# Later places for the normalising, mixing and evacuation of the value chunks, and for two small rows of a decoder layer

## The chip, the cores and the metric

One core of one Trainium2 chip runs the whole layer in one program. The metric is the device time of that program in microseconds. Three runs of the kernel before gave 907.71, 907.95 and 909.17 us, median 907.95.

## The reference

One sequence of 2048 positions with 1024 features goes through one layer:

```
h   = rmsnorm(x, g_pre) * (1 + scale) + shift            # shift, scale, gate from c
u, v, gg, rq, rk, rv, rg = split(h @ w_in)               # seven parts of 512 columns
y_gmlp = u * (tril(W_s) @ layernorm_groups(v) + b) * silu(gg)   # per chunk of 128 positions
y_ret  = groupnorm(retention(rotary(rq), rotary(rk), rv)) * silu(rg)
out = x + gate * rmsnorm(concat(y_gmlp, y_ret) @ w_out, g_post)
```

Layer norm of v takes 4 groups of 128 columns; W_s is a causal 128x128 matrix for each group, applied to the positions inside a chunk. `gate` is a row of 1024 numbers, made from c and a third of w_ada. All of it is float32.

## The kernel before

The sequence is done in two halves of 1024 positions (8 chunks each). Each large product is done as three TensorE products of high and low parts (`mm3`, lines 208 to 210), so each weight block and each activation is first split: ScalarE casts the high part (`wh`, `sh`, `yh`, `hh`), and VectorE subtracts it to get the low part (`wl`, `sl`, `yl`, `hl`). One `mm3` is one step. A half goes through these stages:

1. Retention values, then two passes of queries and keys, a chunk at a time in 8 steps (`token_unit`). `ret_pair` puts the retention of each chunk on the steps behind it: rotate (VectorE), add (GpSimd, L471), transposes `tp` (TensorE, L476), and so on. In half 0 the first four chunks start `6 + 4 * c` steps into the pass.
2. The gMLP values, 8 chunks of 8 steps (`pv`). `v_small` puts five things on the steps behind each chunk: statistics (VectorE, L396 and L398, from PSUM), the root (four small GpSimd instructions, L238, L239, L402, L403), the normalising (four ScalarE instructions, L408, `vh`), the mixing (TensorE, L414, `mx`: four products of 128x128, eight instructions) and its evacuation `into_y` (VectorE, L419, from PSUM). From chunk 2 on, `sums` prepares the sums of activations that stage 3 needs: 32 pieces on VectorE's list (L613, L616, and the splits L601 on ScalarE with L602 on VectorE) and 8 sums on GpSimd (L613), at steps given by SUMS_V and SUMS_G.
3. Six units (`unit`, products X, Y, Z) for the gates and u by a scheme with seven products in place of eight: 28 steps a unit. Weights are split by `pump`, one at the start of each product, more in the last unit; some weight blocks are made on GpSimd (L193, `ut`) first. In half 0 `gate_row` runs beside the units from unit 1 on: four column blocks, each with eight loads `wgt` (SyncE), eight multiply-adds (VectorE, L927 and L929), a split (L936, L937), a `spread` over the partitions (TensorE, L942, `gps`), two loads `gp` and two VectorE operations (L952, L953). The tiles of it share three buffers. In the last unit of half 0, `diag` (VectorE, ten instructions, L250 to L255) and `row` (TensorE, L273, `rb_ps`) spread the 1/rms of half 1's positions; two times, for four chunks each.
4. The output product (`out_unit`, `z`, L967 to L969), 16 steps a chunk. Half 1's h is built beside that of half 0.

The order is written out by hand. `Slots` holds a list of functions by step: `slots.at(d, fn)` puts fn at d steps from now, and `tick`, called ahead of every step, issues what is due. Functions due at the same step are issued in the order in which they were put there. TensorE, VectorE, ScalarE and GpSimd execute their instructions in just this order; a step is thus a place in four queues, not a moment, and an engine that waits for nothing runs ahead of TensorE's steps. `mx`, `gps`, `rb_ps` and `tp` stand in TensorE's queue between the steps: if their input is late, everything behind them on TensorE is late as well.

Of the kernel before, what the change touches and what calls it, by code (L numbers as in the profile page):

```python
# [30 lines left out]
QT = QUAD * P  # L31
XBUF = (9, 3)
OUT_LATE = 8
SUMS_V = ((), (), (1, 3, 4, 5, 6), (1, 3, 4, 5, 6, 7), (1, 3, 4, 5, 6), (1, 3, 4, 5, 6, 7),
          (1, 3, 4, 5, 6), (1, 3, 5, 6, 7))
SUMS_G = ((), (), (0, 5), (4, 6), (4, 6), (4, 6), (), ())
OCH = (4, 5, 6, 7, 0, 1, 2, 3)
V_PUMPS = ((),) * 7 + ((1, 4),)
QK_PUMPS = ((), (), (1,), (1,), (1,), (1,), (1, 4), (1, 4))
# [55 lines left out]
def tile_hybrid_layer(ctx: ExitStack, tc, x, xt, wm, wg, win, wun, wout, wst, cols, rows, pos, cst,  # L95
# [10 lines left out]
    slots = Slots()  # L106
# [29 lines left out]
    def slot(name, shape=(512,), dtype=F32):  # L136
        return big.tile([P, *shape], dtype, name=name, tag="s")
# [99 lines left out]
    def rsqrt_eps(rs, ms, n=1):  # L237
        G.tensor_scalar(rs, ms, 1.0, EPS, ALU.mult, ALU.add)  # L238
        G.tensor_tensor(rs, rs, nhalf[:, 0:n], ALU.pow)  # L239
# [18 lines left out]
    def xpart(half, ch, hf):  # L258
        row = half * HALF + ch * P
        xx = slot("xp")  # L260
        SP.dma_start(xx, x[row:row + P, hf * 512:(hf + 1) * 512])
        jk = slot("xj", dtype=BF16)
        S.activation(jk, xx, AF.Square, scale=1.0 / 32.0, accum_out=ss2[:, hf, ch:ch + 1])
# [21 lines left out]
    def xdma(half, q, kb):  # L285
        t = slot("xt")
        SP.dma_start(t, xt[half * 2 + q, kb])
        return t
# [95 lines left out]

    yT, yR = {}, {}

    def v_small(half, ch, ps, when=(0, 1, 4, 8, 10)):
        mv = small.tile([P, GROUPS, 2], F32, name="mv", bufs=4)
        st = small.tile([P, GROUPS, 6], F32, name="st")
        rs = small.tile([P, GROUPS], F32, name="rsv", bufs=4)  # L390
        nb = small.tile([P, GROUPS], F32, name="nbv", bufs=4)
        box = {}

        def stats():
            for g in range(GROUPS):
                V.bn_stats(st[:, g, :], ps[:, g * P:(g + 1) * P])  # L396
            for g in range(GROUPS):
                V.bn_aggr(mv[:, g, :], st[:, g, :])  # L398

        def root():  # L400
            rsqrt_eps(rs, mv[:, :, 1], GROUPS)
            G.tensor_tensor(nb, mv[:, :, 0], rs, ALU.mult)  # L402
            G.tensor_scalar(nb, nb, -1.0, 1.0, ALU.mult, ALU.mult)  # L403

        def norm():
            vh = box["vh"] = slot("vh", (GROUPS, P))
            for g in range(GROUPS):
                S.activation(vh[:, g, :], ps[:, g * P:(g + 1) * P], AF.Identity,  # L408
                             bias=nb[:, g:g + 1], scale=rs[:, g:g + 1])

        def mix():
            mx = box["mx"] = ps_s.tile([P, GROUPS, P], F32, name="mx", tag="sm")
            for g in range(GROUPS):
                T.matmul(mx[:, g, :], box["vh"][:, g, :], wst_t[:, g, :], start=True, stop=True)  # L414

        def into_y():
            y = yT[half, ch // QUAD]
            for g in range(GROUPS):
                V.scalar_tensor_tensor(y[:, ch % QUAD, g, :], box["mx"][:, g, :],  # L419
                                       cols_t[:, 32 + g:33 + g], bs_b[:, g, :], ALU.mult, ALU.add)  # L420

        for t, fn in zip(when, (stats, root, norm, mix, into_y)):
            slots.at(t, fn)
# [273 lines left out]
    def token_unit(half, ps_i, ch, name, pumps=(1,), pool=None):  # L697
        ps = ps_m.tile([P, 512], F32, name=name, tag="m")
        for kb in range(KB):
            slots.tick()  # L700
            if kb in pumps:
                pump()
            mm3(ps, hchunk(half, ch, kb), blocks[half * PER_HALF + ps_i * KB + kb], kb == 0,
                kb == KB - 1)
        return ps
# [208 lines left out]
    def gate_row(mp):  # L914
        W = 256

        def tile_(name, dtype=F32):
            return mp.tile([P, W], dtype, name=name, tag="w", bufs=3)

        def part(kc, c):  # L920
            a, s1 = gg[:, c * W:(c + 1) * W], sc[:, kc:kc + 1]
            w = tile_("wgt")
            SP.dma_start(w, wg[kc, :, c * W:(c + 1) * W])

            def add():
                if kc == 0:
                    V.tensor_scalar(a, w, s1, None, ALU.mult)  # L927
                else:
                    V.scalar_tensor_tensor(a, w, s1, a, ALU.mult, ALU.add)  # L929

            slots.at(5, add)

        def halves(c):
            a = gg[:, c * W:(c + 1) * W]
            ag[c] = tile_("ah", F32R), tile_("al", F32R)
            S.copy(ag[c][0], a)  # L936
            V.tensor_tensor(ag[c][1], a, ag[c][0].bitcast(F32), ALU.subtract)  # L937

        def spread(c):
            gps[c] = ps_s.tile([P, 512], F32, name="gps", tag="sm")  # L940
            for n in range(2):
                T.matmul(gps[c][:, 0:W], ones_r, ag[c][n], start=n == 0, stop=n == 1)  # L942

        def params(c):
            gp[c] = [tile_("gp") for _ in range(2)]
            for n, t in enumerate(gp[c]):
                at = 512 + n * D + c * W
                SP.dma_start(t, rows[0:1, at:at + W].partition_broadcast(P))

        def end(c):  # L950
            a = gg[:, c * W:(c + 1) * W]
            V.tensor_tensor(a, gps[c][:, 0:W], gp[c][0], ALU.add)  # L952
            V.tensor_tensor(a, a, gp[c][1], ALU.mult)  # L953

        gps, gp, ag = {}, {}, {}
        for c in range(D // W):
            for kc in range(KB):
                slots.at(30 * c + 2 * kc, lambda kc=kc, c=c: part(kc, c))
            for t, fn in ((21, halves), (23, spread), (24, params), (30, end)):
                slots.at(30 * c + t, lambda fn=fn, c=c: fn(c))  # L960

    hb = {}

# [68 lines left out]
    def opened(name):  # L1032
        areas.append(tc.tile_pool(name=name, bufs=1, reuse_waits="tile"))
        return areas[-1].__enter__()
# [10 lines left out]
    qk = {}  # L1045
    for half in range(2):

        if half == 0:
# [3 lines left out]
            rp = opened(f"ret{half}")  # L1052
            table_inputs()
            qk = second_quad(rp, *first)
            for n, fn in enumerate(tables(half, rp)):
                slots.at(n + 2, fn)
        for ch in range(QUAD if half == 0 else 0, NCH):
            ps = token_unit(half, 0, ch, "prv", () if half == 0 else (1,))
            rv_small(half, ch, ps)
            if half == 1 and ch == 2:  # L1060
                closed(3)
                y_tiles("yR", half, yR)
                rp = opened(f"ret{half}")
# [4 lines left out]
        for pr_ in range(2):  # L1068
            early = half == 0 and pr_ == 0
            if early:  # L1070
                for c in range(QUAD):
                    ret_pair(rp, half, pr_, c, qk[c], 6 + 4 * c)
            for ch in range(QUAD if early else 0, NCH):
                if half == 0 and pr_ == 1:
                    for hf in range(2):
                        slots.at(2 + 4 * hf, lambda ch=ch, hf=hf: xpart(1, ch, hf))
                pumps = QK_PUMPS[ch] if pr_ else (1, 4) if early else (1,)
                ps = token_unit(half, 1 + pr_, ch, "pqk", pumps)
                ret_pair(rp, half, pr_, ch, ps, 30 - 4 * ch if early else 0)
# [4 lines left out]
        for ch in range(NCH):  # L1084
            if ch == 2:
                closed()
                y_tiles("yT", half, yT)
                up = opened(f"unit{half}")
                on_v, on_g, late = sums(half, up)
            for t in SUMS_V[ch]:  # L1090
                slots.at(t, on_v.pop(0))
            for t in SUMS_G[ch]:
                slots.at(t, on_g.pop(0))
            ps = token_unit(half, 3, ch, "pv", V_PUMPS[ch])
            v_small(half, ch, ps)


        for un in range(len(UNITS)):
            if un == 0:
                for n, fn in enumerate(late):  # L1100
                    slots.at(1 + 3 * (n // 2) + n % 2, fn)
            if un == 1 and half == 0:
                gate_row(up)
            if un == len(UNITS) - 1:
                slots.at(16, lambda: ysplit(half, OCH[0], 0))
                slots.at(27, lambda: ysplit(half, OCH[0], 1))
            if un == len(UNITS) - 1 and half == 0:
                for q in range(2):
                    def diag(q=q):
                        hb["dg", q] = xdiag2(rs2[:, q * QUAD:(q + 1) * QUAD])  # L1110

                    def row(q=q):
                        hb[q] = xrow(hb["dg", q])

                    slots.at(10 + 6 * q, diag)
                    slots.at(13 + 6 * q, row)

                hb["x"] = []
                for n in range(2):
                    slots.at(24, lambda n=n: hb["x"].append(xdma(1, 0, n)))  # L1120
            unit(half, un, up)
# [82 lines left out]
```

## Time and profile before

| | us |
|---|---|
| median of three runs | 907.95 |
| the profiled execution | 909.25 |
| its span, first to last instruction | 907.5 |
| TensorE (PE) busy | 870.1 |
| VectorE (DVE) busy | 603.7 |
| ScalarE (ACT) busy | 294.3 |
| GpSimd (POOL) busy | 326.8 |

Times in the rows are microseconds from the start of the span. PE stands for TensorE's products, PEld for its weight loads, SPq for SyncE's queue of transfers. A row of a timeline tells in square brackets how long the engine was idle ahead of it and what ended that. `x8` is the number of instructions that a row merges. `hh` is the high, `hl` the low part of h.

### The profile page before, as it was taken

What the parts mean: (1) busy time and instruction counts of PE and PEld (TensorE: products, weight loads), DVE (VectorE), ACT (ScalarE), POOL (GpSimd) and SP (SyncE); (2) the same over time, 40 slices, a digit from 0 to 9 for tenths busy, and PEclk for the clock granted to TensorE, in tenths of its full rate; (3) what the DMA queues carried; (4) which work ended last, traced back from release to release, by engine and by line L of the source; (5) the groups of instructions that cost most, each with busy time, mean ns of one, the idle gap of its engine ahead of it and who ended that gap; (6) DMA issues with size and microseconds to landing.
All of it is one profiled execution on the core that took longest, in us unless ns stands there. A gap on an engine that the chain in (4) does not pass through costs nothing.

```text
span 907.5 us, 11911 instructions
## 1 busy us (share of the span) xinstructions
PE 870.1 (96%) x4198; PEld 717.7 (79%) x4198; DVE 603.7 (67%) x1217; ACT 294.3 (32%) x585; POOL 326.8 (36%) x399
## 2 busy tenths in 40 slices
PE   2999999999899999999999999999998999999997
PEld 1778788888688778778888888888877888888886
DVE  4989876566886777976676665466479734475332
ACT  4673223323263323433351012111124532253221
POOL 2040363356654555311110033333467554630000
PEclk9999999999999999999999999999999999999999
DMA  8961232300012333644443200110001112142222
GB/s 324 333 233 37 92 112 63 97 20 18 1 47 77 104 107 110 248 150 139 152 176 103 81 1 24 59 36 1 1 1 47 47 48 66 56 145 105 95 102 82
DMA packets 43835, 84.86 MB, mean 94 GB/s; under 512 B 5248, under 2 KB 10496, under 8 KB 43776
## 3 DMA queue, kind: packets, MB, share of 16 engines
q1 hardware_dynamic: 43776, 84.10, 27.6%
q8 instruction: 33, 0.54, 0.2%
q14 instruction: 26, 0.21, 0.1%
HBM read 75.69 MB, written 8.39 MB: 93 GB/s over the span
## 4 chain that ended last, share of the span: by engine, by line
PE 74%; DVE 11%; issue 4%; POOL 4%; DMA 3%; ACT 3%; SPq 0%; DVEq 0%; POOLq 0%; ACTq 0%
PE z L968 6%; PE z L969 6%; PE z L967 6%; PE pqk L208 6%; PE pqk L210 6%; PE pqk L209 6%; PE pY L210 3%; PE pY L209 3%; PE pY L208 3%; PE prv L210 2%; PE prv L209 2%; PE prv L208 2%; DVE wl L176 2%; PE o L509 2%; PE pX L209 2%
## 5 line engine op out<-in xcount | busy, mean ns | idle before, releaser
L208 PE MATMUL pqk<-wh,hh 128*128 128x512 f32 x240 | 102.6, 427 | 0.0
L968 PE MATMUL z<-wl,yh 128*128 128x512 f32 (+1 forms) x264 | 101.1, 383 | 0.2 <-DVE wl L176 0.2
L969 PE MATMUL z<-wh,yl 128*128 128x512 f32 (+1 forms) x264 | 101.1, 383 | 0.0
L967 PE MATMUL z<-wh,yh 128*128 128x512 f32 (+1 forms) x264 | 101.0, 383 | 0.0
L210 PE MATMUL pqk<-wh,hl 128*128 128x512 f32 x240 | 94.4, 394 | 0.0
L209 PE MATMUL pqk<-wl,hh 128*128 128x512 f32 x240 | 93.7, 390 | 0.0
L471 POOL TENSOR_TENSOR rA<-rA,rB 128x512 f32<-128x512 f32 x32 | 42.0, 1311 | 134.7 <-DVE rB L463 100.6
L176 DVE TENSOR_TENSOR wl<-wr,wh 128x512 fp32r<-128x512 f32 x94 | 84.3, 920 | 6.5 <-ACT wh L173 6.4
L485 ACT COPY qkT<-tp 128x512 f32<-128x512 f32 x32 | 18.8, 587 | 173.6 <-PE tp L476 173.6
L579 DVE SCALAR_TENSOR_TENSOR zo<-z,zrs,gg 128x512 f32<-128x512 f32 x30 | 22.4, 745 | 58.9 <-POOL zrs L574 58.9
L173 ACT CAST wh<-wr 128x512 fp32r<-128x512 f32 x96 | 55.2, 618 | 17.3 <-DMA wr<-in_win 8.6
L573 POOL TENSOR_SCALAR zrs<-zss 128x1 f32<-128x1 f32 x15 | 4.5, 303 | 148.5 <-ACT jz L570 148.5
L968 PEld LDWEIGHTS z<-wl,yh 128*128 128x128 f32 x264 | 49.6, 188 | 10.2 <-DVE wl L176 0.5
L969 PEld LDWEIGHTS z<-wh,yl 128*128 128x128 f32 x264 | 49.6, 188 | 10.0 <-DVE yl L559 0.4
L967 PEld LDWEIGHTS z<-wh,yh 128*128 128x128 f32 x264 | 49.6, 188 | 9.8
L637 POOL TENSOR_TENSOR yT<-yT,c 128x512 f32<-128x512 f32 x20 | 30.8, 1544 | 62.7 <-DVE c L658 38.7
L210 PEld LDWEIGHTS pqk<-wh,hl 128*128 128x128 f32 x240 | 45.0, 188 | 10.4
L208 PE MATMUL pv<-wh,hh 128*128 128x512 f32 x128 | 52.6, 411 | 0.0
L209 PEld LDWEIGHTS pqk<-wl,hh 128*128 128x128 f32 x240 | 45.5, 189 | 6.5 <-issue 0.2
L210 PE MATMUL pv<-wh,hl 128*128 128x512 f32 x128 | 50.5, 394 | 0.0
L208 PEld LDWEIGHTS pqk<-wh,hh 128*128 128x128 f32 x240 | 45.4, 189 | 6.4 <-issue 0.2
L209 PE MATMUL pv<-wl,hh 128*128 128x512 f32 x128 | 50.4, 394 | 0.0
(233 smaller groups left out, 2216.7 us busy)
## 6 DMA issues: line engine op xcount, KB each, us to landing
wr<-in_win SPq DMA_DIRECT2D x64, 256.0 KB, 3.7
ur<-in_wun SPq DMA_DIRECT2D x48, 256.0 KB, 3.2
slab<-in_wm SPq DMA_DIRECT2D x16, 512.0 KB, 6.7
wr<-in_wout SPq DMA_DIRECT2D x32, 256.0 KB, 4.7
xr<-in_x SPq DMA_DIRECT2D x16, 512.0 KB, 3.4
out<-xr SPq DMA_DIRECT2D x32, 256.0 KB, 2.0
xt<-in_xt SPq DMA_DIRECT2D x24, 256.0 KB, 4.5
xp<-in_x SPq DMA_DIRECT2D x16, 256.0 KB, 2.7
```

The lines of the kernel that those rows point to most:

```text
L173: S.copy(hi, r)
L176: eng.tensor_tensor(lo, r, hi.bitcast(F32), ALU.subtract)
L208: T.matmul(ps, l[0], r[0], start=first, stop=False, skip_group_check=reopened)
L209: T.matmul(ps, l[0], r[1], start=False, stop=False, skip_group_check=reopened)
L210: T.matmul(ps, l[1], r[0], start=False, stop=last, skip_group_check=reopened)
L471: G.tensor_tensor(A, A, box["B"].rearrange("p g h d -> p (g h d)"), ALU.add)
L485: S.copy(qkT, box["tp"])
L579: V.scalar_tensor_tensor(zo, z[c], rs, gg[:, cs], ALU.mult, ALU.mult)
L637: eng.tensor_tensor(y, y, by, ALU.mult)
L967: T.matmul(z, l[0], r[0], start=f, stop=False)
L968: T.matmul(z, l[0], r[1], start=False, stop=False)
L969: T.matmul(z, l[1], r[0], start=False, stop=e)
```

## The change

Numbers in schedules change, nothing else; the instructions are the same.

- `v_small`: normalising at step 7 in place of 4, mixing at 12 in place of 8, `into_y` at 14 in place of 10, counted from the chunk's end. The mixing of a chunk thus goes from the start of the next chunk but one to its middle (step 4 of it).
- SUMS_V: pieces of the sums at steps 1 to 5 (with 7) in place of 1 and 3 to 7. SUMS_G: in two chunks of four the GpSimd sums move from steps 4 and 6 to 5 and 7.
- `gate_row`: 33 steps a block in place of 30; spread at 25 in place of 23, loads `gp` at 26 in place of 24, end at 32 in place of 30.
- `ret_pair` of the first four chunks of half 0: one step later.
- `row` of the roots: 5 steps behind its `diag` in place of 3.

```diff
-SUMS_V = ((), (), (1, 3, 4, 5, 6), (1, 3, 4, 5, 6, 7), (1, 3, 4, 5, 6), (1, 3, 4, 5, 6, 7),
-          (1, 3, 4, 5, 6), (1, 3, 5, 6, 7))
-SUMS_G = ((), (), (0, 5), (4, 6), (4, 6), (4, 6), (), ())
+SUMS_V = ((), (), (1, 2, 3, 4, 5), (1, 2, 3, 4, 5, 7), (1, 2, 3, 4, 5), (1, 2, 3, 4, 5, 7),
+          (1, 2, 3, 4, 5), (1, 2, 3, 5, 7))
+SUMS_G = ((), (), (0, 5), (4, 6), (5, 7), (5, 7), (), ())
...
-    def v_small(half, ch, ps, when=(0, 1, 4, 8, 10)):
+    def v_small(half, ch, ps, when=(0, 1, 7, 12, 14)):
...
-                slots.at(30 * c + 2 * kc, lambda kc=kc, c=c: part(kc, c))
-            for t, fn in ((21, halves), (23, spread), (24, params), (30, end)):
-                slots.at(30 * c + t, lambda fn=fn, c=c: fn(c))
+                slots.at(33 * c + 2 * kc, lambda kc=kc, c=c: part(kc, c))
+            for t, fn in ((21, halves), (25, spread), (26, params), (32, end)):
+                slots.at(33 * c + t, lambda fn=fn, c=c: fn(c))
...
-                    ret_pair(rp, half, pr_, c, qk[c], 6 + 4 * c)
+                    ret_pair(rp, half, pr_, c, qk[c], 7 + 4 * c)
...
-                    slots.at(13 + 6 * q, row)
+                    slots.at(15 + 6 * q, row)
```

## Rows read from the trace of the kernel before

**Rows 1.** The page, part 1: busy time, share of the span, instructions.
```profile
PE 870.1 (96%) x4198; PEld 717.7 (79%) x4198; DVE 603.7 (67%) x1217; ACT 294.3 (32%) x585; POOL 326.8 (36%) x399
```

**Rows 2.** Waits of PE: us in total, times, longest.
```profile
PE mx L414 <- ACT vh L408: 8.0, 6, 1.9
...
PE tp L476 <- POOL rA L471: 1.1, 1, 1.1
PE gps L942 <- DVE al L937: 1.1, 2, 0.6
PE rb_ps L273 <- DVE dgr L254: 1.0, 1, 1.0
...
PE pY L208 <- DVE u L658: 0.7, 1, 0.7
...
PE z L968 <- DVE wl L176: 0.2, 1, 0.2
```

**Rows 3.** Windows from mixing to mixing, half 0: length, PE busy, clock, DMA, GB/s.
```profile
212.14:218.49 6.35, 6.35 (x34) 1.00 0.00 0
...
240.41:249.33 8.92, 7.02 (x32) 1.00 0.00 0
249.33:257.70 8.37, 8.35 (x32) 0.80 0.13 31
```

**Rows 4.** Windows over six such stretches, each half: length, PE, PEld, DVE, ACT, POOL.
```profile
212.14:257.70 45.56, 41.60 (x193) 34.04 (x192) 38.29 (x104) 15.47 (x37) 30.48 (x33) 0.96 0.03 6
653.45:697.53 44.08, 40.05 (x193) 32.82 (x192) 38.05 (x104) 13.96 (x34) 30.52 (x33) 1.00 0.03 7
```

**Rows 5.** Timeline of DVE, value chunks of half 0: start, length, instruction, idle before.
```profile
225.85 0.97 DVE L602 TENSOR_TENSOR sl<-sj,sh 128x512 fp32r<-128x512 f32 x1 [2.42 <-ACT sh L601]
...
233.65 1.56 DVE L602 TENSOR_TENSOR sl<-sj,sh 128x512 fp32r<-128x512 f32 x2 [2.13 <-ACT sh L601]
```

**Rows 6.** Timeline of POOL, same stretch.
```profile
205.84 0.19 POOL L238 TENSOR_SCALAR rsv<-mv 128x4 f32<-128x4 f32 x1 [2.27 <-DVE mv L398]
...
207.51 0.20 POOL L403 TENSOR_SCALAR nbv<-nbv 128x4 f32<-128x4 f32 x1
...
223.73 1.29 POOL L613 TENSOR_TENSOR sj<-hh,hl 128x512 f32<-128x512 f32 x1
...
245.98 2.54 POOL L402 TENSOR_TENSOR nbv<-mv,rsv 128x4 f32<-128x4 f32 x1
```

**Rows 7.** Timeline of ACT, same stretch.
```profile
223.81 1.51 ACT L408 ACTIVATE vh<-pv,nbv,rsv 128x128 f32<-128x128 f32 x4 [4.22 <-POOL nbv L403]
```

**Rows 8.** Windows of units 1 to 5 of half 0: columns as in Rows 4.
```profile
278.80:298.51 19.71, 19.60 (x87) 15.99 (x86) 13.66 (x21) 7.22 (x13) 10.46 (x9) 1.00 0.34 108
298.51:320.23 21.72, 20.17 (x87) 15.84 (x86) 16.11 (x23) 7.22 (x13) 11.63 (x9) 1.00 0.33 105
320.23:341.03 20.80, 19.82 (x87) 15.99 (x86) 16.01 (x24) 6.72 (x12) 11.57 (x9) 1.00 0.33 105
341.03:360.08 19.05, 19.05 (x85) 15.77 (x84) 14.62 (x23) 5.55 (x10) 10.02 (x8) 1.00 0.37 119
360.08:382.05 21.97, 21.00 (x91) 16.67 (x90) 20.49 (x45) 9.13 (x17) 9.18 (x7) 1.00 0.73 264
```

**Rows 9.** Timeline of DVE, unit 2 of half 0.
```profile
311.71 0.48 DVE L929 SCALAR_TENSOR_TENSOR gg<-wgt,sc,gg 128x256 f32<-128x256 f32 x1 [2.58 <-DMA wgt<-in_wg]
312.11 0.68 DVE L658 TENSOR_TENSOR u<-pY,s 128x512 f32<-128x512 f32 x1
```

**Rows 10.** Timeline of DVE, unit 5 of half 0.
```profile
365.97 0.98 DVE L953 TENSOR_TENSOR gg<-gg,gp 128x256 f32<-128x256 f32 x1 [1.38 <-DMA gp<-in_rows]
```

**Rows 11.** Timeline of PE, first query and key chunk behind the start.
```profile
100.51 0.39 PE L210 MATMUL pqk<-wh,hl 128*128 128x512 f32 x1
...
101.19 0.39 PE L210 MATMUL pqk<-wh,hl 128*128 128x512 f32 x1
102.70 0.66 PE L476 MATMUL tp<-cst_t,rA 128*128 128x128 f32 x4 [1.12 <-POOL rA L471]
```

## The prediction

> **What bounds the kernel now.** I read the page's busy shares first: TensorE is busy 96% of the span and VectorE 67% [rows 1], so TensorE's queue is the bound, and an edit that leaves its instructions alone can only win back gaps in it. The waits of TensorE say where the gaps are [rows 2]. The largest within reach is the mixing, which waits 8.0 us on the normalised values, six times; then the spreads of the gate row (the row on `al`, and a like one on `ah`), the roots' row with 1.0, the first transposes of the retention with 1.1, and a product `pY` with 0.7. The list counts only the time ahead of a first instruction, so I take the loss from windows cut at the mixings. An undisturbed stretch from one mixing to the next is 6.35 us; the worst is 8.92, and the one behind it has 8.37 at a mean clock of 0.80 [rows 3]: TensorE fell to its lower level of 1.2 GHz for part of it, right after the longest wait. Six stretches should take 6 x 6.35 = 38.10 us. They take 45.56 in half 0 and 44.08 in half 1 [rows 4]: 7.46 and 5.98 lost, together **13.44 us**, clearly more than the 8.0 of the list.
>
> Why the mixing is late is in the other three queues. ScalarE's normalising stood 4.22 us waiting for GpSimd's `nbv` [rows 7]. Behind it stood the casts `sh`, for which VectorE then idled 2.42 and 2.13 us [rows 5]; behind VectorE stood the next chunk's statistics, thus the next root. So one late chunk makes the next one later, until the pieces of the sums run out.
>
> **The change, part by part.** A step is 0.68 us (101.19 less 100.51) [rows 11].
>
> *Value chunks.* The mixing comes four steps later, 2.72 us more for the same chain. The worst lateness is 8.92 - 6.35 = 2.57 us [rows 3], under 2.72. Normalising at step 7 also lets the casts pass ahead of it on ScalarE, so the two idle times of VectorE and the snowball go. `into_y` is needed only by unit 2's products with yT, so its four steps cost nothing; the mixing in the middle of a chunk writes a PSUM bank of its own and takes TensorE the same time. The gap gone, the clock has no reason to fall. What is late next is VectorE: it is busy 38.29 and 38.05 us in these stretches [rows 4], and they shrink to 38.10. It has no reserve; what does not fit is carried into unit 0, whose weight splits stand in the same queue. Bounds of this give-back: 0 if nothing spills; at most 4.5 us a half if the GpSimd sums that now ran in VectorE's two idle times (four of 1.29 us [rows 6], at most 2.42 + 2.13 = 4.55 of idle [rows 5]) hold VectorE up instead. Since 38.05 against 38.10 is nearly a fit, I take a value near the lower end, 1.0 a half. Sum: 13.44 - 2.0 = 11.4 us won (4.4 to 13.4).
>
> First the row, then a rule on this: a GpSimd root instruction of four columns took 2.54 us at 245.98, its kind 0.20 at best [rows 6], while VectorE was running without a pause. The Trainium skill, "SBUF — State Buffer", section "Who interferes with whom", says why: VectorE and GpSimd share one pair of ports under an exclusive lock, and whoever comes second is blocked for the whole instruction. The trace agrees in kind (2.54 against 0.20). By that rule, closing VectorE's gaps speaks against the change: every sum on GpSimd that used to fall into a gap would now stop VectorE, and the sum would be 4.4 us won in place of 11.4. It is the first rival below.
>
> *Gate row.* Unit 4 has no spread: 19.05 us. Unit 1 has one and waits nowhere by the list: 19.71, so a spread costs up to 0.66 itself. Units 2 and 3 take 21.72 and 20.80 [rows 8], hence 2.01 and 1.09 lost, 3.1 in all. In unit 2, a multiply-add waited 2.58 us for its load, with `u` behind it on VectorE [rows 9] and `pY` behind `u` on TensorE: that is the 0.7 of the list. With 33 steps a block, block 1's adds begin at step 10 of unit 2 in place of 7, the first three of them and the fourth's wait still ahead of `u`; block 2's stand behind it. The spreads fall on step 2 of unit 3, step 7 of unit 4 and step 12 of unit 5, each with 4 steps = 2.72 us between split and spread in place of 1.36; the waits for the two halves of the split are 0.6 at most each on the list [rows 2], so 1.36 more covers them. Of the loads, each multiply-add still frees the buffer for the one three places on, and SyncE stands before a load until then as it does now. Bounds 0 and 3.4 (the latter if a spread costs only 0.35, half of unit 1's excess); I take 2.7, since `pY` of unit 2 may keep a little.
>
> *Roots' row.* Two steps are 1.36 us against a wait of 1.0. But the last unit of half 0 has VectorE busy 20.49 of 21.97 us [rows 8], and block 3 of the gate row now moves into it: four multiply-adds at 0.48 [rows 9] and the split's subtraction, at most 0.98 by the other two-input row of 256 columns [rows 10], make 2.9 us ahead of `diag`. Against that, the block's end, which waited 1.38 us for its load [rows 10], goes behind `diag`, and its load then lands under other work: net at most 1.5 us later. The product `z` already waits for VectorE's splits, 0.2 [rows 2], so what VectorE loses arrives there, and the 1.0 at `rb_ps` isn't won, only moved to `z`. SyncE's load `gp` of block 3 now waits for the spread at step 12, with loads of w_out queued behind it; ScalarE's casts of these run ahead of VectorE, which covers it. Bounds: 1.0 won to 1.5 lost. No row decides between; I take 0.8 lost.
>
> *First retention chunks.* The chain rotate, add, transpose moves as a whole, so its five steps stay five. But VectorE reaches the rotation late (it is still at the tables), so the add ends when it ends, and TensorE does one step more ahead of it: of the 1.1 us wait [rows 2, 11] 0.68 goes. Chunk 4 then follows after 3 steps in place of 4, with its add now ahead of chunk 3's state on GpSimd. Bounds 0 and 0.7; I take 0.7.
>
> **Sum.** 11.4 + 2.7 - 0.8 + 0.7 = 14.0 us. The profiled execution was 909.25 us (span 907.5 and 1.75 around it): it becomes 895.25. The median of the runs is 1.30 under the profiled one, so I forecast 907.95 - 14.0 = **894.0 us**.
>
> **Rivals.**
> 1. *VectorE becomes the bound of value chunks and unit 0.* For: it is busy 38.05 of the 38.10 us that remain, and sums on GpSimd lose the idle time in which they ran. Against: ScalarE's casts no longer make it wait, and the two moved pairs of GpSimd sums fall beside `into_y` and statistics, which read PSUM. Price: 4.5 a half in place of 1.0, 7.0 in all: 901.0 us.
> 2. *The small rows give nothing.* For: the gate row's new phase makes new collisions (block 3 in the unit where VectorE is fullest). Against: twice the distance to each spread. Price: 2.7 not won and 0.7 more lost: 897.4 us.
> 3. *The change doesn't do what it says*: normalising behind the casts comes later by as much as the mixing does, and the gaps stay. Against: the normalising waits for `nbv`, not for its place in the queue [rows 7]. 907.9 us.
> 4. *Slower: the root is held up in every chunk.* The pieces of the sums now stand at steps 1 to 5, right where the root is issued. If two of its instructions are held as the longest row is, 2 x (2.54 - 0.20) = 4.68 us [rows 6], every mixing of the twelve comes 4.68 - 2.72 = 1.96 late: 23.5 us in place of 13.44, the rest as forecast (2.7 - 0.8 + 0.7 won): 907.95 + 10.1 - 2.6 = 915.4 us. Against: of the roots of half 0, one instruction alone was held that long. It decides from (13.44 + 2.6) / 12 = 1.34 us late a mixing on, a root 4.1 us longer than the undisturbed one, which runs from 205.84 to 207.71 [rows 6].
>
> **Chances.** Forecast 0.59, rival 1 0.21, rival 2 0.12, rival 3 0.03, rival 4 0.05. Faster by over 0.2% (1.8 us, about what a measurement of this kernel tells from no change) holds in the first three: 0.92; within it 0.03; slower 0.05. The range goes from 889.0 (nothing given back: 2.0, the gate row's 3.4, the roots' 1.0 won in place of 0.8 lost make 4.5 under 894.0, rounded) to 902.0, which takes in rivals 1 and 2.
>
> **What would show it.** Right: stretches between mixings near 6.35 in both halves, no wait of `mx` on `vh`, no lower clock behind chunk 5, no idle of VectorE on `sh`; units 2 and 3 under 20.2 us; unit 5 and the first `z` product no shorter than before, with `z` waiting on `wl` for longer and `rb_ps` for less; `tp` waiting about 0.4. Rival 1 would show as waits of unit 0's products on `wl` or `u`, rival 4 as root instructions of over 1 us throughout. The prediction fails if waits of `mx` remain above 3 us in all, or if TensorE's new waits on VectorE come to over 5 us.

## The result and the profile after

| | before | after |
|---|---|---|
| median, us (four runs each, one chip) | 908.56 | **895.93** |
| lowest and highest, us | 907.71 to 909.60 | 894.45 to 896.12 |
| ratio, with its 95% interval | | 0.9857 [0.984, 0.9874] |
| span of the profiled execution, us | 907.5 | 894.3 |

The change wins 12.6 us; 14.0 were forecast. The forecast time, 894.0, is 1.9 us short of the median. Two of its terms, though, were wrong by more than that, in opposite directions.

Where the span shrank is read from windows that are cut at the same four places of both kernels: first product of unit 1, first `z`, and first product of unit 1 in half 1. The columns are length, then the busy time of PE, PEld, DVE, ACT and POOL, the granted clock, the DMA share and GB/s. Before:

```profile
0.00:278.80 278.80, 255.35 (x1294) 209.94 (x1295) 206.59 (x468) 108.47 (x213) 112.27 (x162) 0.99 0.33 112
278.80:382.05 103.25, 99.64 (x433) 80.26 (x432) 80.89 (x135) 35.84 (x65) 52.87 (x38) 1.00 0.42 142
382.05:718.90 336.85, 332.38 (x1645) 275.40 (x1644) 229.57 (x486) 92.94 (x189) 104.98 (x148) 1.00 0.21 69
```

After:

```profile
0.00:270.02 270.02, 251.49 (x1294) 208.81 (x1295) 206.00 (x468) 108.26 (x213) 110.47 (x162) 1.00 0.33 116
270.02:375.38 105.36, 100.77 (x433) 81.39 (x432) 86.58 (x134) 35.95 (x65) 53.87 (x38) 0.98 0.40 133
375.38:705.75 330.37, 330.14 (x1645) 275.08 (x1644) 227.80 (x487) 92.69 (x189) 102.39 (x148) 1.00 0.22 72
```

The first and the third stretch, which hold the value chunks of the two halves, win 8.78 and 6.48 us. The second, units 1 to 5 of half 0 with the gate row and the roots' row, **loses 2.11**, although the prediction had 1.9 won there. The remainder of the span differs by 0.05.

The waits of TensorE in the kernel after (us in total, times, longest) answer to [rows 2]:

```profile
...
PE pY L208 <- DVE u L658: 1.9, 2, 1.6
PE gps L942 <- ACT ah L936: 1.6, 1, 1.6
PE gps L942 <- DVE al L937: 0.6, 1, 0.6
PE tp L476 <- POOL rA L471: 0.5, 1, 0.5
PE rb_ps L273 <- DVE dgr L254: 0.4, 1, 0.4
...
PE z L968 <- DVE wl L176: 0.2, 1, 0.2
```

No row on `mx` is left. The same six stretches from mixing to mixing as in [rows 4]:

```profile
213.81:251.88 38.07, 38.07 (x193) 32.40 (x192) 36.45 (x105) 15.27 (x36) 28.56 (x34) 1.00 0.08 27
649.54:687.62 38.08, 38.08 (x193) 32.39 (x192) 36.46 (x105) 15.29 (x36) 28.57 (x34) 1.00 0.09 29
```

TensorE is busy in every microsecond of them, at the full clock. The lengths were 45.56 and 44.08, so 7.49 and 6.00 are won, all that there was to win. The work on VectorE did not become the bound: its busy time fell from 38.29 to 36.45, and GpSimd's from 30.48 to 28.56, with one instruction more on each. So the two are busy for less time with about as much work (not quite the same: VectorE has two sums `sj` of L613 fewer, one split `sl` and two splits `wl` more). Single instructions got longer even so. The splits `sl` of half 0, before and then after (number, busy time in all, mean length in ns, idle time ahead of them and what ended it):

```profile
L602 DVE TENSOR_TENSOR sl<-sj,sh 128x512 fp32r<-128x512 f32 x7 | 5.2, 761 | 4.6 <-ACT sh L601 4.6
L602 DVE TENSOR_TENSOR sl<-sj,sh 128x512 fp32r<-128x512 f32 x8 | 7.8, 979 | 0.0
```

The idle time on `sh` is gone, as forecast.

The loss is in units 4 and 5 (windows of units 1 to 5, columns as above; before in [rows 8]):

```profile
270.02:289.30 19.28, 19.28 (x87) 16.00 (x86) 15.18 (x21) 7.22 (x13) 10.29 (x8) 1.00 0.29 100
289.30:308.50 19.20, 19.20 (x85) 15.69 (x84) 15.80 (x23) 7.13 (x13) 12.17 (x9) 1.00 0.35 112
308.50:327.78 19.28, 19.28 (x87) 16.00 (x86) 15.62 (x22) 5.07 (x9) 10.62 (x8) 1.00 0.43 118
327.78:351.48 23.70, 21.48 (x87) 17.10 (x86) 16.75 (x22) 6.48 (x12) 11.29 (x9) 0.93 0.28 89
351.48:375.38 23.90, 21.53 (x91) 16.59 (x90) 23.22 (x49) 10.03 (x18) 9.49 (x7) 1.00 0.65 232
```

Units 1 to 3 win 0.43, 2.52 and 1.52. Unit 4 loses 4.65 and unit 5 loses 1.93. Unit 4 now has block 2's spread. The timelines there show why it waits (start, length, instruction, idle before it). VectorE:

```profile
323.76 2.95 DVE L929 SCALAR_TENSOR_TENSOR gg<-wgt,sc,gg 128x256 f32<-128x256 f32 x2
327.23 2.37 DVE L929 SCALAR_TENSOR_TENSOR gg<-wgt,sc,gg 128x256 f32<-128x256 f32 x2
...
332.41 1.49 DVE L929 SCALAR_TENSOR_TENSOR gg<-wgt,sc,gg 128x256 f32<-128x256 f32 x1
334.37 0.94 DVE L937 TENSOR_TENSOR al<-gg,ah 128x256 fp32r<-128x256 f32 x1 [0.47 <-ACT ah L936]
```

GpSimd:

```profile
330.27 1.67 POOL L637 TENSOR_TENSOR yT<-yT,c 128x512 f32<-128x512 f32 x1 [0.97 <-DVE c L658]
331.90 1.72 POOL L193 TENSOR_TENSOR ut<-ur 128x512 f32<-128x512 f32 x1
333.57 1.45 POOL L193 TENSOR_TENSOR ut<-ur,ut 128x512 f32<-128x512 f32 x1
```

TensorE, and then the windows (columns as above) over the spread, right behind it and after that:

```profile
334.39 0.38 PE L942 MATMUL gps<-ah,ones 128*128 128x256 f32 x1 [1.63 <-ACT ah L936]
335.36 0.39 PE L942 MATMUL gps<-al,ones 128*128 128x256 f32 x1 [0.59 <-DVE al L937]
```

```profile
332.50:336.50 4.00, 1.78 (x8) 1.17 (x7) 2.33 (x2) 1.93 (x4) 2.52 (x2) 0.99 0.25 38
336.50:341.00 4.50, 4.50 (x14) 3.58 (x13) 2.65 (x5) 0.19 (x1) 0.00 (x0) 0.63 0.89 320
341.00:346.00 5.00, 5.00 (x23) 4.14 (x23) 1.89 (x3) 1.96 (x4) 1.30 (x1) 1.00 0.09 26
```

A multiply-add that took 0.48 us in the kernel before at its best [rows 9] takes 1.2 to 1.5 here (a row of two is read as its mean), five of them, while GpSimd is at `yT` times `c` and at the weight sums `ut`. The kernel before had such long ones in block 2 as well, but two only:

```profile
335.72 2.94 DVE L929 SCALAR_TENSOR_TENSOR gg<-wgt,sc,gg 128x256 f32<-128x256 f32 x2
```

In the kernel after the last one ends at 333.90; TensorE has been standing at the spread since 332.76. It waits 1.63 and 0.59 us, and in the next window the granted clock is 0.63: TensorE spent part of it at 1.2 GHz in place of 2.4, and 14 products pass where 4.50 us at the rate of the window behind it (5.00 us for 23) would pass 20 or 21. In unit 5 the product `pY` waits 1.6 for `u`, which stands on VectorE behind the ten `diag` instructions and block 3 of the gate row. What the longer block was to win in unit 2 is there: no multiply-add waits for its load, and `pY` does not wait for `u`.

### The profile page after: what moved, and what is told of

Same layout as the page of the kernel before. It is cut to its first block, busy times and chain, and to the rows that moved or that the text cites. A ratio compares the mean times of both kernels' runs of the same rounds, so it can differ in the third digit from the quotient of the medians.

```text
span 894.3 us, 11921 instructions
## 1 busy us (share of the span) xinstructions
PE 865.1 (97%) x4198; PEld 717.4 (80%) x4198; DVE 607.3 (68%) x1217; ACT 294.0 (33%) x585; POOL 323.8 (36%) x399
## 4 chain that ended last, share of the span: by engine, by line
PE 86%; DVE 5%; DMA 4%; issue 3%; ACT 1%; SPq 1%; POOL 0%; DVEq 0%; POOLq 0%; ACTq 0%
PE z L969 6%; PE z L968 6%; PE z L967 6%; PE pqk L210 6%; PE pqk L208 6%; PE pqk L209 6%; PE pv L208 3%; PE pv L210 3%; PE pv L209 3%; PE pY L210 3%; PE pY L209 3%; PE pY L208 3%; PE prv L210 2%; PE prv L209 2%; PE prv L208 2%
```

## The experiments

The ratio of each, with its 95% interval, is to the kernel before on the same chip. Times are medians of four to six runs. The experiments ran on four chips, where the kernel before took from 907.94 to 908.81 us, so a difference of two medians from different chips is uncertain by up to 0.9 us; where it is small, that is said. "Units 1 to 5" is the window from the first product of unit 1 to the first `z` in half 0, 103.25 before and 105.36 after.

### Which part of the change does what

**Only the value chunks** (before, with the new steps of `v_small` and the new SUMS_V and SUMS_G, as in the change's diff):

```diff
-    def v_small(half, ch, ps, when=(0, 1, 4, 8, 10)):
+    def v_small(half, ch, ps, when=(0, 1, 7, 12, 14)):
```

> The kernel before with the value chunks' part of the change alone (normalising, mixing, evacuation and the steps of the sums). Theory: this part alone wins 14.2 us, all of the stretches' loss and the waits in unit 0, so 894.3 us; units 1 to 5 as before. Rival, as I predicted it: VectorE gives 2.0 of it back, 897.2 us.

Measured: 894.00 us (893.82 to 894.41), ratio 0.9842 [0.9829, 0.9855]. This part alone wins 14.3 us, 1.9 more than the whole change. I had expected units 1 to 5 as before, but they are 0.92 us shorter. The gate row is untouched here; in its unit 2 VectorE waited 1.97 us for the load for which it waited 2.58 before [rows 9], and the wait of `pY`, 0.7 before, is not in the list. The next experiment, with the same gate row, has it again: 2.56 us for the load and 0.64 at `pY`. So this wait comes and goes. That leaves some 13.4 of the 14.3 to the value chunks, about what the stretches won in the kernel after (7.49 and 6.00). The window of units 1 to 5, and two waits that this kernel keeps from before:

```profile
270.84:373.17 102.33, 99.65 (x433) 80.26 (x432) 82.90 (x135) 35.84 (x65) 53.36 (x38) 1.00 0.43 143
```

```profile
PE tp L476 <- POOL rA L471: 1.1, 1, 1.1
...
PE rb_ps L273 <- DVE dgr L254: 1.0, 1, 1.0
```

**The change without the new gate row:**

```diff
-                slots.at(33 * c + 2 * kc, lambda kc=kc, c=c: part(kc, c))
-            for t, fn in ((21, halves), (25, spread), (26, params), (32, end)):
-                slots.at(33 * c + t, lambda fn=fn, c=c: fn(c))
+                slots.at(30 * c + 2 * kc, lambda kc=kc, c=c: part(kc, c))
+            for t, fn in ((21, halves), (23, spread), (24, params), (30, end)):
+                slots.at(30 * c + t, lambda fn=fn, c=c: fn(c))
```

> The changed kernel with the gate row's old schedule (30 steps a block, spread at 23, end at 30); all else as changed. Theory: the new schedule lost time, since units 1 to 5 of half 0 take 105.4 us in the changed kernel and 103.3 before; with the old one they go back to about 103 us or less (the roots' row keeps its two steps, worth up to 1.0), so 893 to 894 us, some 2 to 3 under the changed kernel; the waits of gps on ah (1.6) and the lower clock in unit 4 go, the waits of units 2 and 3 (2.0 and 1.1) come back. Rival, as I predicted it: the new schedule won 2.7 us, so this kernel takes about 898.6.

Measured: 892.84 us (892.27 to 893.24), ratio 0.9827 [0.9814, 0.984]: 3.1 us **faster** than the whole change. The theory that the new gate row loses holds, the prediction's own term of 2.7 won falls. (By the two ratios the loss is 2.7, and their intervals just touch.)

```profile
270.06:373.16 103.10, 99.43 (x433) 80.25 (x432) 83.08 (x134) 35.75 (x65) 53.79 (x38) 1.00 0.42 142
...
304.34 0.47 PE L208 MATMUL pY<-hh,wh 128*128 128x512 f32 x1 [0.64 <-DVE u L658]
...
367.17 0.47 PE L208 MATMUL pY<-hh,wh 128*128 128x512 f32 x1 [1.46 <-DVE u L658]
```

Against the window of the kernel after, units 1 to 5 are 2.26 us shorter. The other two rows, of the timeline of TensorE, are the wait of unit 2 just spoken of and one in unit 5: the wait of `pY` there is found with the old gate row too, so it belongs to the roots' row. Against the experiment before this one, the retention's step and the roots' row are added. Unit 1 starts 0.78 earlier (270.84 to 270.06: the retention), units 1 to 5 take 0.77 more, and what lies behind the first `z` is 0.8 shorter (519.1 to 518.3: the spans of 892.3 and 891.5 less the ends of the windows). Of the 0.77, the roots' row has 0.5 at most (the 1.0 at `rb_ps` gone, 1.46 at `pY` come); 0.64 is the wait of unit 2, which neither part touches. The two parts were not run apart.

Taken one after the other, the 12.35 us between 908.28, the before of these runs, and 895.93 are 14.3 won with the value chunks, 1.2 by retention and roots' row together, and 3.1 lost by the gate row. The 0.92 of units 1 to 5 is in the first of these figures.

### Value chunks: the sums and the place of the normalising

**The old steps of the sums** (after, with SUMS_V and SUMS_G of before; no other edit):

```diff
-SUMS_V = ((), (), (1, 2, 3, 4, 5), (1, 2, 3, 4, 5, 7), (1, 2, 3, 4, 5), (1, 2, 3, 4, 5, 7),
-          (1, 2, 3, 4, 5), (1, 2, 3, 5, 7))
-SUMS_G = ((), (), (0, 5), (4, 6), (5, 7), (5, 7), (), ())
+SUMS_V = ((), (), (1, 3, 4, 5, 6), (1, 3, 4, 5, 6, 7), (1, 3, 4, 5, 6), (1, 3, 4, 5, 6, 7),
+          (1, 3, 4, 5, 6), (1, 3, 5, 6, 7))
+SUMS_G = ((), (), (0, 5), (4, 6), (4, 6), (4, 6), (), ())
```

> The changed kernel with the old steps of the sums (SUMS_V and SUMS_G as before). Theory: the steps of the sums decide little, since a piece's place is only its order in a queue; stretches between mixings stay at 6.35 us and the time within 1 us of the changed kernel, 895 to 897. Rival: the new steps are what lets VectorE fit; without them mixings or unit 0 wait again by 2 to 4.5 us a half, 900 to 905.

Measured: 898.30 us (898.15 to 899.92), ratio 0.9893 [0.9879, 0.9907], 2.4 more than after. My theory of no more than 1 us falls; the time lies between it and the rival's 900, and what happens is what the rival said. The stretches between mixings stay whole, and the loss is behind them (window, then waits):

```profile
213.56:251.64 38.08, 38.08 (x193) 32.39 (x192) 36.51 (x98) 14.11 (x33) 25.87 (x32) 1.00 0.08 27
```

```profile
PE pY L210 <- DVE wl L176: 0.8, 2, 0.4
```

From the first mixing to unit 1 it takes 58.07 us in place of 56.21, and 1.87 more in half 1 as well. That is the give-back of rival 1: at the window's end VectorE is seven instructions behind (98 in place of 105), and carries them into unit 0, whose products wait for their split weights there. (The list names 0.8 of the 3.7 as waits on `wl`; the rest are delays in unit 0 too short or too spread out to stand in it.) The splits `sl` take 1.18 us on average here, 0.98 in the kernel after. The new steps of the sums avoid the give-back. That 3.7 us in the value stages cost only 2.4 of the time has its reason in unit 4: there the same two waits of 1.6 and 0.6 stand at the spread, but the clock stays up in this profile.

```profile
338.10:342.60 4.50, 4.50 (x21) 3.73 (x20) 2.65 (x5) 1.55 (x4) 0.87 (x1) 1.00 0.92 313
```

21 products pass in a window as long as the one in which 14 passed in the kernel after.

**Only the GpSimd sums at their old steps** (after, with SUMS_G of before):

```diff
-SUMS_G = ((), (), (0, 5), (4, 6), (5, 7), (5, 7), (), ())
+SUMS_G = ((), (), (0, 5), (4, 6), (4, 6), (4, 6), (), ())
```

> The changed kernel with the old steps of GpSimd's sums alone (two chunks at steps 4 and 6 in place of 5 and 7); VectorE's pieces as changed. Tells which of the two lists kept VectorE's work from spilling into unit 0, where the old steps of both cost 1.9 us a half. Theory: VectorE's list did it (its pieces go ahead of the evacuation that waits for TensorE's mixing), so this kernel takes 896 us as the changed one, without a wait of unit 0 on wl. Rival: GpSimd's list did it (its sums now run beside evacuation and statistics, which read PSUM, and don't hold VectorE up); then 898.3 us as with both old.

Measured: 895.51 us (894.17 to 896.27), ratio 0.9854 [0.9834, 0.9875]: as after, and no wait on `wl` in unit 0. So of the two lists, VectorE's, SUMS_V, is the one that counts.

**The normalising back at step 4, the mixing late** (after, with this edit):

```diff
-    def v_small(half, ch, ps, when=(0, 1, 7, 12, 14)):
+    def v_small(half, ch, ps, when=(0, 1, 4, 12, 14)):
```

> The changed kernel with the normalising back at step 4, the mixing left at 12 and the evacuation at 14. Theory: the casts of the sums stand behind the normalising again, so VectorE idles on sh (about 2 us, some twice a half) and its work is late for unit 0; mixings wait under 1 us in all, and the time is 1 to 4 us over the changed kernel, 897 to 900. Rival: the four steps of the mixing are all that counts, and the time is that of the changed kernel within 0.5 us, with no wait in unit 0.

Measured: 902.11 us (898.54 to 903.75), ratio 0.9925 [0.9908, 0.9942]; 6.2 worse than after. The direction held, the price was larger, and its place was another than I had named: no mixing waits, but unit 0 does, on a copy of ScalarE's. The waits of TensorE, then ScalarE's timeline:

```profile
PE pX L208 <- ACT s L673: 3.7, 2, 1.9
```

```profile
255.01 1.51 ACT L408 ACTIVATE vh<-pv,nbv,rsv 128x128 f32<-128x128 f32 x4 [2.49 <-POOL nbv L403]
...
256.91 0.61 ACT L673 COPY s<-pX 128x512 f32<-128x512 f32 x1
```

In the kernel after, the copy at 253.09 runs ahead of the last normalising at 254.08. So the late place is needed for the normalising itself too: ScalarE stands at it until the root is there, and whoever is behind it is late. What the waits do not cover of the 6.2 follows the clock: the run of 898.54 us has a mean of 0.999, that of 903.75 one of 0.993.

### The gate row: length of a block and place of its spread

Two kernels fill the table of the two numbers that the change altered. **Block of 30 with the late spread**, the rest as after:

```diff
-                slots.at(33 * c + 2 * kc, lambda kc=kc, c=c: part(kc, c))
-            for t, fn in ((21, halves), (25, spread), (26, params), (32, end)):
-                slots.at(33 * c + t, lambda fn=fn, c=c: fn(c))
+                slots.at(30 * c + 2 * kc, lambda kc=kc, c=c: part(kc, c))
+            for t, fn in ((21, halves), (25, spread), (26, params), (30, end)):
+                slots.at(30 * c + t, lambda fn=fn, c=c: fn(c))
```

> The changed kernel with 30 steps a block in the gate row as before, but its spread at 25 and its loads gp at 26 as changed (end at 30). Tells the block's length apart from the spread's distance. Theory: the length did the harm (it puts block 2's last multiply-add and split at the start of unit 4, where GpSimd is busiest) and the distance helps: the waits of gps on ah and al in units 2 and 3 (about 1.0 each with spread at 23) go, units 1 to 5 take 101 us in place of 103.1, the time is 891 us. Rival: the distance does nothing, since the split comes as much later as it may; 892.8 us, as with the old schedule.

**Block of 33 with the early spread** (and its `params` and `end` as before), the rest as after:

```diff
-            for t, fn in ((21, halves), (25, spread), (26, params), (32, end)):
+            for t, fn in ((21, halves), (23, spread), (24, params), (30, end)):
```

> The changed kernel with 33 steps a block in the gate row, but spread at 23, loads gp at 24 and end at 30 as before. Theory: the length of 33 does the harm, and with two steps less the wait of gps in unit 4 is 1.4 us longer (about 3 on ah), units 1 to 5 take 106 to 108 us, the time is 897 to 898. Rival: the distance did the harm (loads gp behind the spread hold up the queue of transfers), so the time falls to 893.

Measured, with the two kernels that were there already (the block's end is at 32 in the kernel after and at 30 in the other three):

| | spread at 23 | spread at 25 |
|---|---|---|
| block of 30 steps | 892.84 | 890.89 (890.46 to 891.98), ratio 0.9811 [0.9797, 0.9824] |
| block of 33 steps | 899.42 (898.69 to 900.05), ratio 0.9902 [0.9888, 0.9916] | 895.93 |

Both expectations held in the time, the second with 1.4 us more than I had; with the block of 30 one spread still waits 0.5 on `al`. The distance wins 2.0 at the one length and 3.5 at the other; the longer block loses 5.0 or 6.6. Block of 33, spread at 23, the longest wait of all of them:

```profile
PE gps L942 <- ACT ah L936: 4.3, 2, 3.0
```

**Is it GpSimd that makes the multiply-adds long?** After, with three products `yT` times `c` of unit 3 in half 0 on VectorE in place of GpSimd; each costs VectorE 0.69 us. The products with `c21` and `c12` get the same condition as this one:

```diff
-        slots.at(0, lambda: used(half, kind, pair, up, tmp["c22"], 1, 1, False))
+        slots.at(0, lambda: used(half, kind, pair, up, tmp["c22"], 1, 1, False, half == 0 and un == 3))
```

> The changed kernel with three multiplications of yT by u in unit 3 of half 0 (128x512, 1.5 to 1.7 us each on GpSimd, around the start of unit 4) moved from GpSimd to VectorE, where such a one takes about 0.7. Adds 2 us to VectorE's own work, takes 4.8 from GpSimd. Theory: VectorE's multiply-adds of the gate row's block 2 were long (about 1.5 us in place of 0.48) because GpSimd ran beside them, so with fewer GpSimd instructions there the split is ready sooner: the wait of gps on ah in unit 4 falls from 1.6 to under 0.8 and the lower clock goes, 893 to 895 us. Rival: the multiply-adds are late by their place in VectorE's queue; 2 us more work ahead of them makes the wait 2 us longer, 898 us.

Measured: 891.95 us (891.43 to 892.52), ratio 0.982 [0.9804, 0.9836], 4.0 less than after. VectorE has more instructions, and the block is ready earlier:

```profile
327.62 1.00 DVE L929 SCALAR_TENSOR_TENSOR gg<-wgt,sc,gg 128x256 f32<-128x256 f32 x2
...
330.94 0.48 DVE L929 SCALAR_TENSOR_TENSOR gg<-wgt,sc,gg 128x256 f32<-128x256 f32 x1
331.88 0.43 DVE L937 TENSOR_TENSOR al<-gg,ah 128x256 fp32r<-128x256 f32 x1 [0.47 <-ACT ah L936]
```

The same instructions as in the kernel after take 1.00 for two in place of 2.37, 0.48 in place of 1.49 and 0.43 in place of 0.94, and no spread waits. GpSimd is idle beside them, for 10.78 us up to this row:

```profile
336.87 1.30 POOL L637 TENSOR_TENSOR yT<-yT,sg 128x512 f32<-128x512 f32 x1 [10.78 <-ACT sg L645]
```

That settles it: the length of the multiply-adds was GpSimd's work beside them. The traces of all 13 kernels agree. Of their multiply-adds of L929, the 201 that overlap no GpSimd instruction took 0.47 to 0.49 us without exception; every longer one, up to 1.60, ran beside GpSimd.

### The roots' row, and the pieces put together

**`diag` earlier** (after with the old gate row, and the two `diag` at step 12 of units 3 and 4 in place of steps 10 and 16 of the last unit; the `row` stays):

```diff
+            if un in (3, 4) and half == 0:
+                def diag(q=un - 3):
+                    hb["dg", q] = xdiag2(rs2[:, q * QUAD:(q + 1) * QUAD])
+
+                slots.at(12, diag)
...
-                    slots.at(10 + 6 * q, diag)
```

> The changed kernel with the gate row's old schedule, and the two diag of the roots' row moved out of the last unit of half 0, to step 12 of units 3 and 4 (each ten VectorE instructions, 1.9 us); the rows stay. Takes 3.8 us of VectorE's work out of unit 5. Theory: VectorE's fullness in unit 5 is what the roots' row stumbled over; the wait of pY on u there (1.5 us) goes, with no new wait at rb_ps or z, so 891 us. Rival: pY waits for something else (a load, ScalarE), or VectorE only moves the wait to units 3 and 4; 892.8 us as without it.

Measured: 891.57 us (890.88 to 892.17), ratio 0.9817 [0.9803, 0.9831]; 1.3 less than with `diag` late, on another chip (the runs of the two kernels do not overlap; by the ratios it is 0.9). No wait of `pY`, `rb_ps` or `z` is left in unit 5 (the wait of unit 2, which this edit does not touch, is not in this profile either). So that loss came from VectorE's queue in the fullest unit, not from the distance between `diag` and `row`.

**Both**, the block of 30 with its spread at 25 and `diag` early (the two diffs together):

> The two together: 30 steps a block with spread at 25, and the two diag at step 12 of units 3 and 4. Theory: the gains add, 889 to 890 us, about 6 under the changed kernel. Rival: both lean on the same idle time of VectorE in units 3 and 4, and the sum is no better than the better of the two, 891.

Measured: **889.53 us** (888.89 to 890.30), ratio 0.9794 [0.978, 0.9808], the best of all, 6.4 under the change:

```profile
269.97:369.32 99.35, 98.67 (x433) 80.05 (x432) 84.97 (x136) 36.35 (x67) 53.91 (x38) 1.00 0.43 147
```

TensorE is idle for 0.68 of 99.35 us there; in the kernel after it is for 4.59 of 105.36.

**The three products on VectorE as well** (that kernel with the diff of the three products):

> All that helped, together: 30 steps a block with the spread at 25, the two diag at step 12 of units 3 and 4, and the three multiplications by u of unit 3 of half 0 on VectorE. Theory: what is left of the spread's waits around unit 4 (0.9 on the second part of the split) goes too, since GpSimd no longer runs beside that split: 888 to 889 us, about 7 under the changed kernel. Rival: with both diag and the three multiplications VectorE is now too full in units 3 and 4, and pY waits for u there: 890 us or more.

Measured: 894.73 us (894.30 to 895.47), ratio 0.9857 [0.984, 0.9873]; 5.2 worse. My theory falls. The rival's time holds; the cause is in the timelines of TensorE, VectorE and GpSimd:

```profile
327.64 0.47 PE L208 MATMUL pY<-hh,wh 128*128 128x512 f32 x1 [3.72 <-DVE u L658]
```

```profile
321.01 1.32 DVE L254 TENSOR_SCALAR dgr<-cst_t,rsh 128x128 fp32r<-128x128 f32 x1
...
326.81 0.68 DVE L658 TENSOR_TENSOR u<-pY,s 128x512 f32<-128x512 f32 x1
```

```profile
320.89 1.35 POOL L193 TENSOR_TENSOR ut<-ur,ut 128x512 f32<-128x512 f32 x1
322.21 1.28 POOL L193 TENSOR_TENSOR ut<-ur 128x512 f32<-128x512 f32 x1
```

With three products fewer, GpSimd runs ahead and comes to its `ut` while VectorE is at `diag`. A `dgr` of 0.28 us takes 1.32, four of the eight do so, `u` stands behind them, and TensorE waits 3.72 for it. Behind this wait the granted clock is 0.62 over 4.50 us (327.64 to 332.14), which is most of the rest of the 5.2.

## Why the prediction came out, point by point

**Value chunks: right in the mechanism, too small by 2.9** (11.4 forecast, 14.3 alone on the chip). Everything that it named is there: stretches of 6.35 us, no wait of `mx`, no idle time on `sh`, no fall of the clock. The term that failed is the give-back of 1.0 a half, 2.0 of the 2.9: nothing is given back. It was taken from 38.05 busy against 38.10, as if the busy time would stay; it fell to 36.45. The other 0.9 are those of units 1 to 5, the wait of `pY` behind a load, which the prediction had in the gate row's term. And the steps of the sums, for which I had no term, are what prevents it: with the old ones it is 1.9 a half, inside my bounds of 0 to 4.5.

Rival 1 would have shown as waits of unit 0 on `wl` or `u`; there are none. Its loss exists, but with the old steps of the sums alone. Rival 4 did not come either: the four instructions of a root take 2.7 us on average in half 0's stretches after and 3.1 before. I had drawn rival 1 from the Trainium skill ("SBUF — State Buffer", section "Who interferes with whom"): VectorE and GpSimd lock each other out for whole instructions, so sums without a gap to run in would stop VectorE. The trace of these stretches as a whole does not agree, since the busy time of both engines went down; for `sl` alone it does (0.76 us on average before, 0.98 after, 1.18 with the old steps of the sums).

**Gate row: wrong in its sign** (2.7 won forecast, 3.1 lost). Units 2 and 3 came under 20.2 us as I had said, the wait of `pY` in unit 2 is gone, and the spreads did fall on the steps named. The step that failed is "1.36 more covers them": it took the lateness of the split from the waits of before, 0.6 at most, and carried it over to other steps. What the two more steps give was right, 2.0 to 3.5 us by the table; what three steps more a block take, 5.0 to 6.6, was not in the sum. They shift block 2's last five multiply-adds to where GpSimd runs beside VectorE with one pause of 0.97 us. About half of the 3.1 seems to hang on the clock: by the one run of the kernel after with a mean clock of 0.999, 894.45 us, the loss is 1.6. I had written that "the gate row's new phase makes new collisions", under rival 2, and put it at nothing won, not at a loss of 3.1. (The term's upper bound was added up wrongly as well: two units at 0.31 more each make 3.7, not 3.4.)

The same section of the Trainium skill has a rule for this one: a VectorE instruction that reads two tensors from SBUF contends with a GpSimd instruction that reads there, and the one that starts second is blocked. The trace agrees: the multiply-add reads `wgt` and `gg`, and took 1.49 beside GpSimd and 0.48 without.

**Roots' row: the direction right, the place not.** The wait did move rather than go, but to `pY` (1.46 us, for `u` behind `diag`), not to `z`, whose wait stays at 0.2. Units 1 to 5 took 0.77 more beside the old gate row, which looks like the forecast 0.8, but that is luck: 0.64 of it is the wait of unit 2, and 1.46 less 1.0 leaves 0.5 at most for this part. Behind the first `z` 0.8 came back, which I had not counted; in that run the row of `z` is gone from the list.

**Retention: right.** 0.7 forecast, 0.78 measured; the wait of `tp` went from 1.1 to 0.5.

**Sum.** The error of the gate row, 5.8, is made up by 2.9 of the value chunks and 1.3 of the two small terms (1.2 won, 0.1 lost forecast); 1.6 remain of the gain. That the time came out near the forecast proves none of its terms: only taking the parts apart showed that one of them had the wrong sign. What would have falsified the prediction, 3 us of waits on the mixing or 5 us of new waits on VectorE, did not come; the list of waits could not show the gate row's loss whole, since the clock's part of it is no wait.

**Left open:** why the clock fell behind the spread in the kernel after and not with the old sums, after the same two waits. The runs of the kernel after that ended at 895.82 to 896.12 have a mean clock of 0.997, and the one at 894.45 has 0.999, so it is not the same in every execution. The kernel with GpSimd's sums at their old steps has the same two waits and times of both kinds (896.27 and 896.10 at 0.997, 894.91 and 894.17 at 0.999). Its profile is of the slowest of them, and the clock falls at the same place:

```profile
336.50:341.00 4.50, 4.50 (x16) 3.58 (x15) 2.65 (x5) 0.07 (x1) 0.00 (x0) 0.70 0.88 308
```

So the steps of the sums need not be what decides; an execution may or may not have the fall.

## What to carry to other kernels

In a kernel whose order is written by hand, a step is a place in every queue: before moving one, list for its new place what the other engines run beside it, and take an instruction's length from there, not from where it stood. When a change has several parts, run them apart: here the best version takes the longer block back and `diag` out of the fullest unit. And where a wait ends at an engine, look first at what stands ahead in its queue; giving that work an earlier place (about 1.3 us for `diag`) did more for the roots' row than more distance behind it.

## What the runs showed of the hardware

- The multiply-adds of 128x256 on VectorE took 0.48 us alone and mostly 1.2 to 1.5 beside GpSimd's sums and products of 128x512; even a `dgr` with one tensor of 128x128 took 1.32 in place of 0.28.
- Moving 3 instructions from GpSimd to VectorE cost 5.2 us in one kernel and won 4.0 in another, by where its next ones fell.
- After two waits of 1.63 and 0.59 us TensorE's granted clock was 0.63 over 4.5 us in one profile and 0.70 in another, and 1.00 in that of a third kernel after waits as long. The runs of the first with a mean clock of 0.997 are some 1.5 us longer than the one with 0.999 (896.0 against 894.45); that the fall lies at the same place in each of them is not shown, as one of them alone was profiled.
